# Expert v products of a two-block transformer layer: the weights go into the array and the tokens stream

## The chip, the core and the metric

One core of a Trainium2 chip runs the kernel. TensorE (PE; its weight loads are listed as PEld), VectorE (DVE), ScalarE (ACT), GpSimd (POOL) and SyncE (SP, which issues the DMAs) work side by side and meet at semaphores. The metric is the device time of one execution in microseconds (us); the median of several executions is given. The spread of the executions of this kernel is small, so a change of 0.2% can be told from none.

## What is computed

The program runs two transformer blocks on 256 tokens of width 1024. The change lies in the last layer of the first block and at the start of the second. The first block's feed-forward picks, for every token and each of 8 heads, 16 of 16384 experts; an expert has a row u and a row v of 1024 numbers.

```
def peer_ffn(h, w_query, sub_keys_1, sub_keys_2, expert_u, expert_v):
    ...
        g = jax.nn.softmax(best, axis=-1)
        u = expert_u[idx]
        act = jax.nn.gelu(jnp.einsum('td,thkd->thk', xc, u).astype(jnp.float32), approximate=False)
        w = (g * act).astype(h.dtype)
        return jnp.einsum('thk,thkd->td', w, expert_v[idx])
...
    x = x + peer_ffn(rms_norm(x, ffn_norm_g[layer]), ...)
return rms_norm(x, final_norm_g)
```

The second block begins with two sums over the width of that result, a root-mean-square norm of its own and a product with its first weights (`w_in_e_2`), whose columns feed a short convolution in time.

## The kernel before

**Experts as dense products.** The gather is replaced by products over all experts. They are cut into 64 units of 256 experts. Unit u of index j (`unit_u`, `wstat`, L230) computes gelu(u.x) for 256 experts and 256 tokens. Unit v of index j (`unit_v`, L726) multiplies this by the gate weights `gts`, which a one-hot stage has written to HBM (`gd`) and 16 DMAs of 64 KB bring back for every 4 units, and then by the 256 rows of v (`vstat`, L256). All products are done in three passes of the type float32r: each operand is split into a high part (ACT copy, L77 or L737) and a low part (DVE subtraction, L78 or L738), and high*high, high*low and low*high are summed in PSUM (`mm3`, L82).

**Two ways to place the operands.** In `wstat` the weights are the array's stationary operand, 128x128 at a time, and the tokens stream, 256 columns; one u unit is 48 matmuls of 256 columns (lines L240 to L242). In `vstat` the gated activations `wh`/`wl` are the stationary operand and the rows of v stream, 512 columns; one v unit is 24 matmuls of 512 columns (L83 to L85). Its four accumulators `pv` (tokens x width) fill the four banks of the pool `acc` over all 64 units.

**Order of the work.** A scheduler lays the instructions of each engine out from the program text, and each engine then takes its own list in order. Units u28 to u33 stand one behind the other, then v0, u34, v1, u35 and so on up to u63, v30, and then v31 to v63 alone. The second block's feed-forward (tile names `m`) has the same two kinds of unit: `m_0`*n*`p` (first layer) and `m_1`*n*`p` (second layer) with 48 matmuls of 256 streamed columns, each followed by `m` with 24 of 512.

**Which tokens stream.** In the u units, in the convolution's units `cv0` to `cv5` and in `m_0` the streamed tokens are the tiles `gh`/`gl`; in `m_1` they are `bh`/`bl`. In the built program these tiles begin, in each partition, at byte 22272 and 30464 (`gh`, `gl`), 107680 and 115872 (`bh`, `bl`), and 200864, 202912, 204960 and 207008 (the two buffers each of `wh` and `wl`). The first two are multiples of 64; the others all leave a remainder of 32. The buffers of the split weights (72256, 80448, 88640, 96832) are multiples of 64.

**After v63.** Four DVE additions (L748) put the sum on the residual `x`. Eight PE transposes a half (L92, `prep_half`) turn `x` into width x tokens, ACT and DVE split it (L100, L101), and `cv0` and `cv1` multiply it with the first weights. Beside that `factors` takes the sums of squares (DVE L792, eight ACT passes L794) and a chain of small DVE operations up to `rr` (L803), which `rb` and the convolution's first operation (`cvb`, L831) need. `cv0` uses a bank of the pool `acc`, which the accumulators leave free.

Of the kernel before, what the change touches and what calls it, by code (L numbers as in the profile page):

```python
# [10 lines left out]
F32 = mybir.dt.float32  # L11
# [5 lines left out]
AF = mybir.ActivationFunctionType  # L17
OP = mybir.AluOpType
# [3 lines left out]
P = 128  # L22
T = 256
D = 1024
# [24 lines left out]
def kernel(ctx: ExitStack, tc: tile.TileContext, A: dict, out: bass.AP):  # L49
    nc = tc.nc  # L50
    V, S, PE, GP = nc.vector, nc.scalar, nc.tensor, nc.gpsimd
# [7 lines left out]
    def acc_tile(name):  # L59
        return acc.tile([P, 512], F32, tag="acc", name=name)  # L60

    def mm_tile(name):
        return mmp.tile([P, 512], F32, tag="mm", name=name)
# [18 lines left out]
    def mm3(o, ah, al, bh, bl, start, stop):  # L82
        PE.matmul(o, ah, bh, start=start, stop=False)  # L83
        PE.matmul(o, ah, bl, start=False, stop=False)  # L84
        PE.matmul(o, al, bh, start=False, stop=stop)  # L85

    def prep(src, nk, gain, hi, lo, k0=0, full=None, pool=mm_tile):

        for k in range(nk):
            pt = pool(f"pt{k}")  # L90
            for t in range(2):
                PE.transpose(pt[:, t * P : t * P + P], src[t][:, k * P : k * P + P], ident)  # L92
            if gain is None:
                a = S.activation(hi[:, k0 + k], pt[:, :T], AF.Copy)
                v = V.tensor_sub(lo[:, k0 + k], pt[:, :T], hi[:, k0 + k].bitcast(F32))
            else:
                g = gain(k)
                if full is not None:
                    S.activation(full[:, k0 + k], pt[:, :T], AF.Copy, scale=g)
                a = S.activation(hi[:, k0 + k], pt[:, :T], AF.Copy, scale=g)  # L100
                v = V.scalar_tensor_tensor(lo[:, k0 + k], pt[:, :T], g, hi[:, k0 + k].bitcast(F32), OP.mult, OP.subtract)  # L101
        return a, v
# [71 lines left out]
    def load_ahead(src, n, name, after=(), dst=None):  # L174
        if name not in ahead:
            ahead[name] = load_split(src, n, name, after, dst)
# [8 lines left out]
    def fetch(src, n, name):  # L185
        return ahead.pop(name) if name in ahead else load_split(src, n, name)
# [69 lines left out]
    def vstat(ah, al, src, accs, first, last, name):  # L256

        hi, lo = fetch(src, 2048, name)
        order = [(j, t, nh) for j in range(2) for t in range(2) for nh in range(2)]
        if last:  # L260
            order = [(j, t, nh) for nh in range(2) for t in range(2) for j in range(2)]
        for j, t, nh in order:
            c = slice(j * D + nh * 512, j * D + nh * 512 + 512)
            a = slice(j * T + t * P, j * T + t * P + P)
            mm3(accs[t][nh], ah[:, a], al[:, a], hi[:, c], lo[:, c], first and j == 0, last and j == 1)


    c0 = const.tile([P, C0_COLS], F32, name="c0")
    fin = const.tile([P, D], F32, name="fin")
# [3 lines left out]
    ident = c0[:, C_ID : C_ID + P]  # L273
# [4 lines left out]
    x = [const.tile([P, D], F32, name=f"x{t}") for t in range(2)]  # L278
# [36 lines left out]
    with tc.tile_pool(name="p1", bufs=1) as p1:  # L315
        xh, xl = gh, gl_
# [148 lines left out]
        yT, last_exp = {}, []  # L465
# [67 lines left out]
    with tc.tile_pool(name="p2", bufs=1) as p2, tc.tile_pool(name="gdram", bufs=1, space=bass.MemoryType.DRAM) as gdp:  # L533
        gd = [gdp.tile([P, P, 16], F32, name=f"gd{i}") for i in range(16)]
        xh, xl = gh, gl_
# [8 lines left out]
        def unit_u(n=1, xf=None):  # L544
            for _ in range(n):
                j = nu[0]
                if j == 64:
                    return
                nu[0] += 1
                ps = wstat(xh, xl, A["eu"][j], f"u{j}") if xf is None else wstat_f32(xf, A["eu"][j], f"u{j}")  # L550
                g = p2.tile([P, 512], F32, tag="ga", name=f"ga{j}", bufs=NG)
                S.activation(g, ps, AF.Gelu)
                gact[j] = g
# [3 lines left out]
        with tc.tile_pool(name="p2a", bufs=1) as p2a:  # L557
            rs_f, pr = [], []
# [13 lines left out]
            def split_x():  # L572
                for k in range(0, 8, 2):
                    S.activation(xh[:, k : k + 2], xf[:, k : k + 2], AF.Copy)
                    V.tensor_sub(xl[:, k : k + 2], xf[:, k : k + 2], xh[:, k : k + 2].bitcast(F32))
# [117 lines left out]
        with tc.tile_pool(name="p2c", bufs=1) as p2c:  # L693

            for b in range(16):
                unit_u(1)
                stg = p2c.tile([P, P, 16], F32, tag="stg", name=f"stg{b}", bufs=2)
                for q in range(2):
# [11 lines left out]
                    for g in range(2):  # L710
                        ps = acc_tile(f"gp{b}{q}{g}")
                        for i in range(4):
                            for m in range(2):
                                PE.matmul(ps[:, i * P : i * P + P], oh[0][:, g, :, i], oh[2 + m][:, g, :, i], start=m == 0,  # L714
                                          stop=m == 1)
                        c = q * 8 + g * 4
                        S.activation(stg[:, :, c : c + 4], ps.rearrange("p (t n) -> p n t", t=4), AF.Copy,  # L717
                                     scale=2.0 ** -15)
# [1 line left out]

        p2x.__exit__(None, None, None)
        with tc.tile_pool(name="p2b", bufs=1) as p2b:
            accs = [[acc_tile(f"pv{t}{nh}") for nh in range(2)] for t in range(2)]
            gts = {}

            def unit_v(j):  # L726
                q, jj = divmod(j, 4)
                if jj == 0:
                    gts[q] = p2b.tile([P, 16, 8, 16], F32, tag="gt", name=f"gt{q}", bufs=2)
                    for i in range(16):  # L730
                        nc.sync.dma_start(gts[q][:, i], gd[i][:, 8 * q : 8 * q + 8, :])
                w = gact.pop(j)
                w4 = w.rearrange("p (j g t) -> p j g t", j=2, g=16)
                V.tensor_tensor(w4, w4, gts[q][:, :, 2 * jj : 2 * jj + 2, :].rearrange("p g j t -> p j g t"), OP.mult)  # L734
                wh = p2b.tile([P, 512], F32R, tag="wh", name=f"wh{j}", bufs=2)
                wl = p2b.tile([P, 512], F32R, tag="wl", name=f"wl{j}", bufs=2)
                S.activation(wh, w, AF.Copy)  # L737
                V.tensor_sub(wl, w, wh.bitcast(F32))  # L738
                vstat(wh, wl, A["ev"][j], accs, j == 0, j == 63, f"v{j}")

            unit_u(6)
            for j in range(64):
                unit_v(j)
                unit_u()
            for nh in range(2):
                for t in range(2):
                    c = slice(nh * 512, nh * 512 + 512)
                    V.tensor_add(x[t][:, c], accs[t][nh], x[t][:, c])  # L748


    with tc.tile_pool(name="p3", bufs=1) as p3:
        h = x
        xh, xl = gh, gl_
# [11 lines left out]
        def p4(name, bufs=2, tag=None):  # L765
            return p3.tile([P, 4, P], F32, tag=tag or name[:-1], name=name, bufs=bufs)
# [11 lines left out]
        gg = p3.tile([P, 8], F32, name="gg")  # L778
        V.tensor_mul(gg, gcols[:, G_FIN : G_FIN + 8], gcols[:, G_LME : G_LME + 8])
        rr = sm.tile([P, 2], F32, tag="rr", name="rr")  # L780

        def prep_half(hf):
            c = slice(hf * 512, hf * 512 + 512)
            return prep([x[t][:, c] for t in range(2)], 4, lambda k: gg[:, 4 * hf + k : 4 * hf + k + 1], xh, xl, k0=4 * hf)

        def factors():
            ss4 = sm.tile([P, 2, 2, 2], F32, tag="ss4", name="ss4")
            for hf in range(2):
                for t in range(2):
                    c = slice(hf * 512, hf * 512 + 512)  # L790
                    tt = t1[t][:, c]
                    V.tensor_mul(tt, x[t][:, c], fin[:, c])  # L792
                    for i, z in enumerate((x[t][:, c], tt)):
                        S.activation(mm_tile(f"s3{i}{t}{hf}"), z, AF.Square, accum_out=ss4[:, i, t, hf : hf + 1])  # L794
            ss = sm.tile([P, 4], F32, tag="ss4s", name="ss4s")
            rf = sm.tile([P, 4], F32, tag="rf", name="rf")
            V.tensor_add(ss.rearrange("p (a t) -> p a t", a=2), ss4[:, :, :, 0], ss4[:, :, :, 1])

            V.tensor_scalar(ss, ss, 1.0 / D, None, OP.mult)
            V.tensor_scalar(ss[:, 0:2], ss[:, 0:2], EPS, None, OP.add)  # L800
            V.scalar_tensor_tensor(ss[:, 2:4], ss[:, 0:2], EPS, ss[:, 2:4], OP.mult, OP.add)
            rsqrt(rf, ss, 1.0, 0.0, 4, "rf")
            V.tensor_copy(rr, rf[:, 2:4])  # L803
            scale_row()
            return rf

        rb = p3.tile([P, T], F32, name="rb")
        kqT = p3.tile([P, 8, T], F32, tag="kqT", name="kqT")
        kT, qT = kqT[:, 0:4], kqT[:, 4:8]
        tok = {p: [p4(f"{p}tok{t}", tag="vb" if p == "q" else None) for t in range(2)] for p in "kvq"}  # L810
        ktok, vtok = tok["k"], tok["v"]
        ba = p3.tile([P, 2, 8], F32, name="ba")
# [9 lines left out]
        def conv_mm(u, at=None):  # L822
            return wstat(xh, xl, A["w_conv"][u], f"cv{u}", acc_tile, at)
# [47 lines left out]
        def w_uvz(n):  # L871
            gemm(xh, xl, A["w_uvz"], 8, [(n, k) for k in range(2)], evac_uvz, name="wu")

        prep_half(0)
        pr = []
        cps = [conv_mm(0, lambda: pr.extend(prep_half(1)))]
        load_ahead(A["w_conv"][1], 2048, "cv1", pr)
        rf = factors()
        nc.sync.dma_start(c2, A["c2"])
        V.tensor_copy(nmask, c2[:, C_STR : C_STR + 2 * P].rearrange("p (a b) -> p a b", a=2))  # L880
        V.tensor_scalar(nones, ones, -1.0, None, OP.mult)
# [27 lines left out]
        al = sm.tile([P, 4], F32, tag="al", name="al", bufs=1)  # L909
# [59 lines left out]
        for t in range(2):  # L969
# [4 lines left out]
            for i, (one, col) in enumerate(((nones, gc), (ones, ngc))):  # L974
# [3 lines left out]
                d = p4(f"de{i}{t}", 1)  # L978
# [4 lines left out]
            tt = slice(t * P, t * P + P)  # L983
# [3 lines left out]
            a = p4(f"am{t}")  # L987
# [77 lines left out]
        o = [p4(f"o{t}", tag="w1_1") for t in range(2)]  # L1065
        st = None
        for c in range(4):
            t, r0 = c // 2, c % 2 * 64
# [452 lines left out]
```

## Time and profile before

| | us |
|---|---|
| median of 3 executions | 1773.56 |
| lowest, highest | 1773.37, 1774.61 |
| the profiled execution | 1775.11 |
| its span, first to last instruction | 1773.3 |
| PE busy | 1731.5 (98%) |
| DVE busy | 1132.5 (64%) |
| ACT busy | 886.1 (50%) |

The rows come from the profiled execution, whose clock starts with the span. Matmuls are pipelined: a row gives 0.39 us for one of 512 columns though the next starts 0.23 us later. So times of PE are read here from the starts of units, not from the durations.

### The profile page before, as it was taken

The numbers are of one execution on the slowest core, as the hardware profiler recorded it, in microseconds if no ns is written. First come the engines' busy times: TensorE is split into PE (matmuls) and PEld (weight loads), VectorE is DVE, ScalarE is ACT, GpSimd is POOL, SyncE is SP. The second block draws the span as 40 slices with busy tenths as digits, with TensorE's granted clock in tenths as the row PEclk, the third lists the DMA queues.
The fourth block names the chain that finished last, engine by engine and source line by source line (L and its number), as shares of the span: only waits on it lengthen the run. The fifth ranks groups of instructions, "written<-read, shape, count | busy, mean of one in ns | idle before, by whom it ended". The sixth has DMA issues, their size and how long they took to land.

```text
span 1773.3 us, 26306 instructions
## 1 busy us (share of the span) xinstructions
PE 1731.5 (98%) x10702; PEld 1522.5 (86%) x10702; DVE 1132.5 (64%) x1924; ACT 886.1 (50%) x1156; POOL 22.9 (1%) x22
## 2 busy tenths in 40 slices
PE   8999999999999999999999999999999999999998
PEld 7788899999999999999888888887999787789996
DVE  6646689978646565555555578666555676765555
ACT  5765543544544444444444458545444557554444
POOL 0000000000000000000000000001000001100000
PEclk9999999999999999999999999999999999999999
DMA  6424445465677777775555553215555553345552
GB/s 236 140 96 161 157 156 203 157 227 224 220 246 243 246 250 247 247 239 191 186 184 188 187 185 126 99 50 178 190 189 191 172 182 127 115 171 185 179 185 93
DMA packets 83067, 321.40 MB, mean 181 GB/s; under 512 B 9473, under 2 KB 44545, under 8 KB 47105
## 3 DMA queue, kind: packets, MB, share of 16 engines
q1 hardware_dynamic: 82944, 319.71, 52.9%
q8 instruction: 84, 1.38, 0.3%
q14 instruction: 39, 0.31, 0.0%
HBM read 301.85 MB, written 17.83 MB: 180 GB/s over the span
## 4 chain that ended last, share of the span: by engine, by line
PE 89%; DVE 6%; ACT 3%; issue 1%; DMA 0%; SPq 0%; DVEq 0%; ACTq 0%
PE pv L85 7%; PE pv L83 7%; PE pv L84 7%; PE gp L714 3%; PE m L84 3%; PE m L83 3%; PE m L85 3%; PE wia L83 1%; PE wia L84 1%; PE wia L85 1%; PE pt L92 1%; PE pj L1181 1%; PE wua L85 1%; PE wda L85 1%; PE wda L84 1%
## 5 line engine op out<-in xcount | busy, mean ns | idle before, releaser
L737 ACT ACTIVATE wh<-ga 128x512 fp32r<-128x512 f32 x64 | 40.4, 632 | 194.8 <-PE pv L84 194.8
L738 DVE TENSOR_TENSOR wl<-ga,wh 128x512 fp32r<-128x512 f32 x64 | 44.2, 692 | 90.7 <-ACT wh L737 90.7
L714 PE MATMUL gp<-oh,oh 128*128 128x128 f16 x512 | 63.5, 297 | 0.0
L714 PEld LDWEIGHTS <-oh 128*128 128x128 f16 x512 | 57.5, 117 | 1.5
L1201 ACT ACTIVATE ah<-mr 128x512 fp32r<-128x512 f32 x32 | 20.2, 631 | 76.8 <-DVE mr L1198 76.8
L709 DVE TENSOR_TENSOR oh<-oh,gT 128x1024 f16<-128x1024 f16 x64 | 42.3, 687 | 23.9 <-PE gp L714 23.9
L734 DVE TENSOR_TENSOR ga<-ga,gt 128x512 f32<-128x512 f32 x64 | 41.1, 686 | 2.9 <-DMA gt<-gd 2.8
L1202 DVE TENSOR_TENSOR al<-mr,ah 128x512 fp32r<-128x512 f32 x32 | 22.2, 692 | 21.6 <-ACT ah L1201 21.6
L717 ACT ACTIVATE stg<-gp 128x512 f32<-128x512 f32 x64 | 34.8, 600 | 1.7 <-PE gp L714 1.2
L92 PE MATMUL pt<-c,x 128*128 128x128 f32 x128 | 21.7, 296 | 7.4 <-DMA x<-x 5.9
L92 PEld LDWEIGHTS pt<-c,x 128*128 128x128 f32 x128 | 16.1, 150 | 12.7 <-issue 6.0
L706 DVE TENSOR_TENSOR oh<-iotaR,i1T 128x1024 f16<-128x1024 f16 x32 | 22.1, 689 | 5.1 <-PE gp L714 3.7
L78 DVE TENSOR_TENSOR wiw_0l<-wiw,wiw_0h 128x2048 fp32r<-128x2048 f32 x7 | 16.0, 2292 | 12.7 <-ACT wiw_0h L77 12.7
L100 ACT ACTIVATE gh<-pt,gcols 128x256 fp32r<-128x256 f32 x32 | 13.0, 475 | 19.4 <-PE pt L92 19.4
L84 PE MATMUL wia<-wiw_0l,gh 128*128 128x512 f32 x56 | 22.5, 402 | 0.0
L85 PE MATMUL wia<-wiw_0h,gl 128*128 128x512 f32 x56 | 22.5, 401 | 0.0
L83 PE MATMUL wia<-wiw_0h,gh 128*128 128x512 f32 x56 | 22.3, 404 | 0.0
L83 PE MATMUL wia<-wiw_1h,gh 128*128 128x512 f32 x56 | 22.0, 392 | 0.0
L85 PE MATMUL wia<-wiw_1h,gl 128*128 128x512 f32 x56 | 21.9, 392 | 0.0
L84 PE MATMUL wia<-wiw_1l,gh 128*128 128x512 f32 x56 | 21.9, 392 | 0.0
L1198 DVE TENSOR_TENSOR mr<-mr 128x512 f32<-128x512 f32 x32 | 21.9, 685 | 0.0
L101 DVE SCALAR_TENSOR_TENSOR gl<-pt,gcols,gh 128x256 fp32r<-128x256 f32 x32 | 13.6, 478 | 12.2 <-ACT gh L100 12.2
(2944 smaller groups left out, 6680.2 us busy)
## 6 DMA issues: line engine op xcount, KB each, us to landing
u<-eu SPq DMA_DIRECT2D x64, 1024.0 KB, 4.9
v<-ev SPq DMA_DIRECT2D x64, 1024.0 KB, 4.9
m<-w_mlp SPq DMA_DIRECT2D x64, 1024.0 KB, 4.8
gd<-stg SPq DMA_DIRECT2D x16, 1024.0 KB, 3.9
gt<-gd SPq DMA_DIRECT2D x256, 64.0 KB, 4.4
wiw<-w_in SPq DMA_DIRECT2D x14, 1024.0 KB, 5.4
wdw<-w_qkv SPq DMA_DIRECT2D x12, 1024.0 KB, 4.8
q<-w_query SPq DMA_DIRECT2D x8, 1024.0 KB, 5.1
```

What stands on the lines that cost most here:

```text
L83: PE.matmul(o, ah, bh, start=start, stop=False)
L84: PE.matmul(o, ah, bl, start=False, stop=False)
L85: PE.matmul(o, al, bh, start=False, stop=stop)
L92: PE.transpose(pt[:, t * P : t * P + P], src[t][:, k * P : k * P + P], ident)
L706: V.tensor_tensor(oh[0], io, tok(i1T), OP.is_equal)
L709: V.tensor_tensor(oh[2 + i], oh[1], tok(gT[i]), OP.mult)
L714: PE.matmul(ps[:, i * P : i * P + P], oh[0][:, g, :, i], oh[2 + m][:, g, :, i], start=m == 0, stop=m == 1)
L717: S.activation(stg[:, :, c : c + 4], ps.rearrange("p (t n) -> p n t", t=4), AF.Copy, scale=2.0 ** -15)
L734: V.tensor_tensor(w4, w4, gts[q][:, :, 2 * jj : 2 * jj + 2, :].rearrange("p g j t -> p j g t"), OP.mult)
L737: S.activation(wh, w, AF.Copy)
L738: V.tensor_sub(wl, w, wh.bitcast(F32))
L1202: V.tensor_sub(al, r, ah.bitcast(F32))
```

## The change

The v products now place their operands like the u products: 128x128 blocks of v are stationary, and the gated activations `wh`/`wl` stream with all 256 tokens. The sum so stands as width x tokens, in four banks `yT`, two blocks of 128 of the width in each. It begins with the residual: 16 matmuls of `x` with the identity (`residual_t`) write the transposed `x` into the banks before v0. After v63 ACT and DVE split the banks directly (`split_x`), and ACT also copies them to `xT`; `factors` transposes `xT` back on PE and takes its sums from PSUM.

```diff
+    def vstat_t(ah, al, src, accs, last, name):
+
+        hi, lo = fetch(src, 2048, name)
+        for d in range(8):
+            o = accs[d // 2][:, d % 2 * T : d % 2 * T + T]
+            for j in range(2):
+                c = slice(j * D + d * P, j * D + d * P + P)
+                a = slice(j * T, j * T + T)
+                PE.matmul(o, hi[:, c], ah[:, a], start=False, stop=False, skip_group_check=True)
+                PE.matmul(o, hi[:, c], al[:, a], start=False, stop=False, skip_group_check=True)
+                PE.matmul(o, lo[:, c], ah[:, a], start=False, stop=last and j == 1, skip_group_check=True)
...
-            accs = [[acc_tile(f"pv{t}{nh}") for nh in range(2)] for t in range(2)]
+
+
             gts = {}
+
+            def residual_t():
+                for m in range(4):
+                    for i in range(4):
+                        d, t = 2 * m + i // 2, i % 2
+                        PE.matmul(yT[m][:, i * P : i * P + P], x[t][:, d * P : d * P + P], ident, start=i == 0, stop=False,
+                                  skip_group_check=True)
...
-                vstat(wh, wl, A["ev"][j], accs, j == 0, j == 63, f"v{j}")
+                vstat_t(wh, wl, A["ev"][j], yT, j == 63, f"v{j}")
 
             unit_u(6)
+            yT = [acc_tile(f"pv{m}") for m in range(4)]
+            residual_t()
             for j in range(64):
                 unit_v(j)
                 unit_u()
-            for nh in range(2):
-                for t in range(2):
-                    c = slice(nh * 512, nh * 512 + 512)
-                    V.tensor_add(x[t][:, c], accs[t][nh], x[t][:, c])
...
-        def prep_half(hf):
-            c = slice(hf * 512, hf * 512 + 512)
-            return prep([x[t][:, c] for t in range(2)], 4, lambda k: gg[:, 4 * hf + k : 4 * hf + k + 1], xh, xl, k0=4 * hf)
+        def split_x():
+
+            for m in range(4):
+                for k in (2 * m, 2 * m + 1):
+                    o = yT[m][:, k % 2 * T : k % 2 * T + T]
+                    S.activation(xh[:, k], o, AF.Copy, scale=gg[:, k : k + 1])
+                    V.scalar_tensor_tensor(xl[:, k], o, gg[:, k : k + 1], xh[:, k].bitcast(F32), OP.mult, OP.subtract)
+                last = S.activation(xT[:, 2 * m : 2 * m + 2], yT[m].rearrange("p (k t) -> p k t", k=2), AF.Copy)
+            return last
...
                     tt = t1[t][:, c]
-                    V.tensor_mul(tt, x[t][:, c], fin[:, c])
-                    for i, z in enumerate((x[t][:, c], tt)):
-                        S.activation(mm_tile(f"s3{i}{t}{hf}"), z, AF.Square, accum_out=ss4[:, i, t, hf : hf + 1])
+                    xp = mm_tile(f"xp{t}{hf}")
+                    for k in range(4):
+                        PE.transpose(xp[:, k * P : k * P + P], xT[:, 4 * hf + k, t * P : t * P + P], ident)
+                    V.tensor_mul(tt, xp, fin[:, c])
+                    for i, z in enumerate((xp, tt)):
+                        S.activation(xp, z, AF.Square, accum_out=ss4[:, i, t, hf : hf + 1])
...
-        prep_half(0)
-        pr = []
-        cps = [conv_mm(0, lambda: pr.extend(prep_half(1)))]
+        pr = [split_x()]
+        cps = [conv_mm(0)]
```

On PE the first rows of unit v20 before were these; the name ahead of the arrow is the accumulator, behind it stand the streamed operand and the stationary one, and then the shape of the output.

```order
L83 MATMUL pv00_5098<-v20h_7393,wh20_7387 128x512
L84 MATMUL pv00_5098<-v20l_7394,wh20_7387 128x512
L85 MATMUL pv00_5098<-v20h_7393,wl20_7388 128x512
L83 MATMUL pv01_5099<-v20h_7393,wh20_7387 128x512
L84 MATMUL pv01_5099<-v20l_7394,wh20_7387 128x512
L85 MATMUL pv01_5099<-v20h_7393,wl20_7388 128x512
```

With the change the same place on PE reads:

```order
L275 MATMUL pv0_5440<-wh20_7883,v20h_7889 128x256
L276 MATMUL pv0_5440<-wl20_7884,v20h_7889 128x256
L277 MATMUL pv0_5440<-wh20_7883,v20l_7890 128x256
L275 MATMUL pv0_5440<-wh20_7883,v20h_7889 128x256
L276 MATMUL pv0_5440<-wl20_7884,v20h_7889 128x256
L277 MATMUL pv0_5440<-wh20_7883,v20l_7890 128x256
```

The two operands have changed places, the streamed one is half as wide, and a unit has 48 such rows in place of 24. The tiles `wh` and `wl` keep the byte addresses given above.

On ACT, between v63 and the first weights of the second block, these rows stood before (`gh` is the high part of the transposed sum, `pt` a bank with transposes, `gg` a gain):

```order
L77 ACTIVATE cv0h_9721<-cv0_9719 128x2048
L100 ACTIVATE gh_72<-pt0_9699,gg_9685 128x256
L100 ACTIVATE gh_72<-pt1_9704,gg_9685 128x256
L100 ACTIVATE gh_72<-pt2_9709,gg_9685 128x256
L100 ACTIVATE gh_72<-pt3_9714,gg_9685 128x256
...
L77 ACTIVATE cv1h_9796<-cv1_9794 128x2048
L794 ACTIVATE s3000_9802,ss4_9800<-x0_76 128x512
```

With the change ACT's list there is (`pv0` to `pv3` are the banks of the sum):

```order
L77 ACTIVATE cv0h_11269<-cv0_11267 128x2048
L805 ACTIVATE gh_72<-pv0_5440,gg_11233 128x256
L805 ACTIVATE gh_72<-pv1_5441,gg_11233 128x256
L805 ACTIVATE gh_72<-pv2_5442,gg_11233 128x256
L805 ACTIVATE gh_72<-pv0_5440,gg_11233 128x256
L805 ACTIVATE gh_72<-pv3_5443,gg_11233 128x256
L805 ACTIVATE gh_72<-pv1_5441,gg_11233 128x256
L805 ACTIVATE gh_72<-pv2_5442,gg_11233 128x256
L807 ACTIVATE xT_11237<-pv0_5440 128x512
L807 ACTIVATE xT_11237<-pv1_5441 128x512
L807 ACTIVATE xT_11237<-pv2_5442 128x512
L805 ACTIVATE gh_72<-pv3_5443,gg_11233 128x256
```

The copy of `pv0` to `xT` stands behind seven high parts, one of which reads `pv3`, the bank that v63 fills last. The accumulator of `cv0` gets the bank of `pv0`, and its first matmul waits for that copy.

On PE the 16 transposes between v63 and `cv1`, half of which stood ahead of `cv0` and half among its matmuls, now stand behind `cv0`:

```order
L241 MATMUL cv0p_11273<-gl_73,cv0h_11269 128x256
L242 MATMUL cv0p_11273<-gh_72,cv0l_11270 128x256
L819 MATMUL xp00_11329<-c0_70,xT_11237 128x128 x4
L819 MATMUL xp10_11337<-c0_70,xT_11237 128x128 x4
L819 MATMUL xp01_11345<-c0_70,xT_11237 128x128 x4
L819 MATMUL xp11_11353<-c0_70,xT_11237 128x128 x4
L240 MATMUL cv1p_11395<-gh_72,cv1h_11324 128x256
```

## Rows read from the trace of the kernel before

**Rows 1.** The page's part 4: the chain that ended last, share by engine.
```profile
PE 89%; DVE 6%; ACT 3%; issue 1%; DMA 0%; SPq 0%; DVEq 0%; ACTq 0%
```

**Rows 2.** Busy time by stretch: us, PE, PEld, DVE, ACT, POOL, PEclk, DMA share, GB/s.
```profile
519.00:851.00 332.00, 332.00 (x2159) 299.31 (x2158) 193.49 (x149) 144.84 (x120) 0.00 (x0) 1.00 0.72 237
857.00:1042.00 185.00, 185.00 (x792) 148.71 (x791) 99.34 (x68) 79.62 (x65) 0.00 (x0) 1.00 0.55 187
1080.00:1090.00 10.00, 6.99 (x37) 6.18 (x36) 9.92 (x29) 7.25 (x16) 0.10 (x1) 0.76 0.18 46
1575.00:1735.00 160.00, 160.00 (x993) 143.51 (x992) 83.00 (x57) 69.88 (x58) 0.00 (x0) 1.00 0.55 185
```

**Rows 3.** Timeline of PE, first matmuls of v0, v17, u51, v18: start, us.
```profile
518.46 0.39 PE L83 MATMUL pv<-v0h,wh 128*128 128x512 f32 x1
...
706.93 0.39 PE L83 MATMUL pv<-v17h,wh 128*128 128x512 f32 x1
...
712.55 0.28 PE L240 MATMUL u51p<-gh,u51h 128*128 128x256 f32 x1
...
718.02 0.39 PE L83 MATMUL pv<-v18h,wh 128*128 128x512 f32 x1
```

**Rows 4.** Timeline of PE, first matmuls of u29, u30, u31.
```profile
490.19 0.28 PE L240 MATMUL u29p<-gh,u29h 128*128 128x256 f32 x1
...
495.85 0.28 PE L240 MATMUL u30p<-gh,u30h 128*128 128x256 f32 x1
...
501.50 0.28 PE L240 MATMUL u31p<-gh,u31h 128*128 128x256 f32 x1
```

**Rows 5.** Timeline of PE, the feed-forward's units: ends of m_05p, m_11p, m_112p.
```profile
1260.59 0.28 PE L240 MATMUL m_05p<-gh,m_05h 128*128 128x256 f32 x1
...
1266.06 0.39 PE L83 MATMUL m<-m_05h,ah 128*128 128x512 f32 x1
...
1564.04 0.28 PE L240 MATMUL m_11p<-bh,m_11h 128*128 128x256 f32 x1
...
1569.80 0.28 PE L240 MATMUL m_12p<-bh,m_12h 128*128 128x256 f32 x1
...
1683.50 0.28 PE L240 MATMUL m_112p<-bh,m_112h 128*128 128x256 f32 x1
...
1689.26 0.39 PE L83 MATMUL m<-m_112h,ah 128*128 128x512 f32 x1
```

**Rows 6.** Timeline of PE: matmuls of x with a diagonal, float32, 128 columns.
```profile
209.41 3.81 PE L569 MATMUL ptn<-dgf,x 128*128 128x128 f32 x32 [2.49 <-issue]
```

**Rows 7.** Timeline of PE from v63 to cv2: start, us, count.
```profile
1036.60 0.40 PE L83 MATMUL pv<-v63h,wh 128*128 128x512 f32 x1
...
1042.23 1.04 PE L92 MATMUL pt<-c,x 128*128 128x128 f32 x8
1043.84 0.39 PE L240 MATMUL cv0p<-gh,cv0h 128*128 128x256 f32 x1 [0.57 <-ACT gh L100]
...
1057.82 0.39 PE L240 MATMUL cv2p<-gh,cv2h 128*128 128x256 f32 x1 [0.53 <-ACT cv2h L77]
```

**Rows 8.** Timeline of ACT over the same stretch.
```profile
1043.31 1.57 ACT L100 ACTIVATE gh<-pt,gg 128x256 fp32r<-128x256 f32 x4 [4.59 <-PE pt L92]
...
1049.29 0.61 ACT L794 ACTIVATE s<-x 128x512 f32<-128x512 f32 x1
```

**Rows 9.** Timeline of DVE over the same stretch.
```profile
1054.33 0.16 DVE L797 TENSOR_TENSOR ss4s<-ss 128x4 f32<-128x4 f32 x1 [1.85 <-ACT s L794]
...
1057.60 0.17 DVE L803 COPY rr<-rf 128x2 f32<-128x2 f32 x1
...
1061.26 2.28 DVE L78 TENSOR_TENSOR cv3l<-cv,cv3h 128x2048 fp32r<-128x2048 f32 x1
...
1063.73 0.68 DVE L831 TENSOR_TENSOR cvb<-cv0p,rb 128x512 f32<-128x512 f32 x1
...
1070.75 0.70 DVE L934 TENSOR_SCALAR x<-uv,rf 128x1024 f32<-128x1024 f32 x1
```

More of the change, by code (lines that the diff above doesn't have):

```diff
@@ L807 @@
         rb = p3.tile([P, T], F32, name="rb")
-        kqT = p3.tile([P, 8, T], F32, tag="kqT", name="kqT")
-        kT, qT = kqT[:, 0:4], kqT[:, 4:8]
+        xT = p3.tile([P, 8, T], F32, tag="kqT", name="xT")
         tok = {p: [p4(f"{p}tok{t}", tag="vb" if p == "q" else None) for t in range(2)] for p in "kvq"}
@@ L872, in w_uvz @@
             gemm(xh, xl, A["w_uvz"], 8, [(n, k) for k in range(2)], evac_uvz, name="wu")
-        prep_half(0)
-        pr = []
-        cps = [conv_mm(0, lambda: pr.extend(prep_half(1)))]
+        pr = [split_x()]
+        cps = [conv_mm(0)]
         load_ahead(A["w_conv"][1], 2048, "cv1", pr)
         rf = factors()
+        kqT = p3.tile([P, 8, T], F32, tag="kqT", name="kqT")
+        kT, qT = kqT[:, 0:4], kqT[:, 4:8]
         nc.sync.dma_start(c2, A["c2"])
```

## The prediction

> **What bounds the kernel now.** I read the chain that ended last first: 89% of it is PE [rows 1]. Then the busy time by stretch, for the stretch that is changed: from 519 to 851 us, where u and v units alternate, and from 857 to 1042 us, where v units stand alone, PE is busy without a gap, its granted clock is 1.00 (2.4 GHz), DVE is busy for 58% and 54% and ACT for 44% and 43% [rows 2]. So the time of the expert products is the sum of PE's matmul intervals, and nothing that ACT, DVE or the queues do there shows, as long as it keeps up. Last I read where units start on PE, since durations of pipelined matmuls do not add up. v17 takes 712.55 - 706.93 = 5.62 us for 24 matmuls of 512 columns, 234 ns each; u51 takes 718.02 - 712.55 = 5.47 us for 48 of 256 columns, 114 ns each [rows 3]. From the first v0 to the end of v63 it is 1042.23 - 518.46 = 523.77 us [rows 3, 7]; less 30 u units at 5.475 that leaves 5.62 us for each of 64 v units. Each unit computes the same number of products, so on this alone the new form, which has the shape and the count of a u unit, would gain. The reader is to see that this is not the only interval which the trace has for that shape.
>
> **The v units: which interval.** Three intervals stand in the trace for 48 float32r matmuls of 256 streamed columns, all at clock 1.00. With `gh`/`gl` streaming, u51 takes 5.47 us and m_05p 1266.06 - 1260.59 = 5.47 us [rows 3, 5]. With the same tiles u29 and u30 take 5.66 and 5.65 us [rows 4]. With `bh`/`bl` streaming, m_11p takes 1569.80 - 1564.04 = 5.76 us and m_112p 1689.26 - 1683.50 = 5.76 us [rows 5]. m_05p and m_112p do the same work on the same buffers of split weights and stand in the same alternation with units of 512 columns; what differs is the streamed tile. `gh`/`gl` begin at a byte that is a multiple of 64, `bh`/`bl` 32 bytes past one, and `wh`/`wl`, which now stream, also 32 past one. m_11p follows another unit of 256 columns, as every v unit now does, and it too takes 5.76 us. So the nearest row for the new v unit is m_11p, not u51. I take 5.76: 0.14 us more than now, times 64 is **+9.0 us**. The bounds are u51's 5.47 (-0.15 x 64 = -9.6, or -9.0 with the mean of 5.62 and u's 5.48) and m_11p's own 5.76; u30's 5.655 in between gives +2.3.
>
> The Trainium skill speaks against this reading of the addresses: "SBUF — State Buffer", section Specifications, gives lines of 16 bytes as what an access crosses, and 32 bytes past a multiple of 64 is the start of such a line. By it the new v units would run as u51 does, and the sum of this term would be -9.0 us. No row here shows why `bh`/`bl` stream at 5.76 us; the address is what I find to differ, and it may not be the reason.
>
> **The u units between them.** The 30 units u34 to u63 stand in the same place as before and stream `gh`/`gl`. But this form has two intervals, 5.47 and 5.65, and units that follow one another at 5.65 stay there: u29 and u30 do, and both run at clock 1.00. Now u units follow a v unit that is itself of 256 columns. Below, they stay at 5.475: no cost. Above, all 30 go to 5.655: 30 x 0.18 = +5.4 us. I take 0, since u51 and m_05p enter 5.47 from another form each time, and keep +5.4 as a case of its own.
>
> **The residual at the start.** 16 float32 matmuls of 128 columns stand on PE between u33 and v0, which followed one another without a gap. The same operation with another right side is `x` with a diagonal: 32 in 3.81 us, the last of which ends 0.28 us after it starts, so 3.81 less that pipeline end is 0.11 us each [rows 6]. 16 x 0.11 = **+1.8 us**. Nothing covers it, since PE is the bound there. Below it is nothing only if PE had idled before v0, and it did not. The four DVE additions after v63 go; what they gave back is counted next.
>
> **After v63.** I count from the first matmul of v63 (1036.60) [rows 7]. Before, PE ended v63 at 5.63, ran eight transposes, started `cv0` at 7.24 and `cv2` at 21.22, and `cvb`, behind which DVE works nearly without a gap (9.92 of 10 us between 1080 and 1090 [rows 2]), came at 27.13 [rows 9]. With the change: the last bank is filled at 5.76, ACT sees it at about 6.0, does three high parts at 0.39 (four take 1.57 [rows 8]) and the copy of `pv0` at 0.61, and `cv0`, which waits for that copy, starts at 7.9. **This is a new wait**, and the whole of PE's list stands behind it. `cv0` runs without stops at 5.45 to 13.4; 16 transposes at 0.11 follow to 15.2; `cv1` ends at 20.7, against 21.2. So PE has lost nothing there. But the sums of squares now wait for the transposes, and before them stands the split of `cv2`'s weights, whose buffer is free when `cv0` ends: 13.4 + 2.1 = 15.5. Eight passes at 0.61 [rows 8] end at 20.4, and the chain to `rr` takes 1057.60 - 1054.33 = 3.3 [rows 9]: 23.7, where it was 21.0, 2.7 us later. What DVE does between `rr` and `cvb` changes too: one split of 2.28 (`cv2l`) now stands ahead of `rr`, and the scaling of the second half of `x` (0.70, at 1070.75 before) comes ahead of `cvb` [rows 9]. So `cvb` comes at 27.13 + 2.7 - 2.3 + 0.7 = 28.2, with 0.7 us of later work already done and 0.14 counted with v63: **+0.3**, which I round to **+0.5 us** for one more handover between engines. Bounds: -1 (if PE's start sets the rest) to +2.7 (if the whole delay of `rr` stays). The additions taken away are worth nothing beyond that, since `cv0` waits for ACT in their place.
>
> ACT and DVE hide the rest: a v unit still has one split of weights and one of activations. From 519 to 851 us, 60 units, that is 144.84 / 60 = 2.4 us of ACT and 193.49 / 60 = 3.2 us of DVE a unit [rows 2], within 5.5. No DMA is added or moved.
>
> **Sum.** 9.0 + 1.8 + 0.5 = +11.3 us. On the span of 1773.3 that gives 1784.6, on the execution's own 1775.11 it gives 1786.4; the median of the runs shown lies 1.55 below that execution, so I say **1784.9 us**.
>
> **Rivals.**
> 1. The u units fall to 5.655 too: 11.3 + 5.4 = +16.7, 1790.3. For it: all that follows u28 at that interval stays there [rows 4]. Against: 30 u units now enter 5.47 within their first matmuls after v.
> 2. The new v units run like u51, and the kernel is faster: -9.0 + 1.8 + 0.5 = -6.7, 1766.9. It decides from a v unit below 5.58 us on, where 64 x 0.04 pays for the residual and the end. For it: the same shape, weights and buffers as u. Against: both units named with a tile 32 bytes past a multiple of 64 take 5.76. This is also what the Trainium skill's page named above would make of it.
> 3. The v units run like u30: +2.3 + 1.8 + 0.5 = +4.6, 1778.2. For it: u's second interval needs no odd address. Against: m_05p and m_112p differ though they are entered alike.
> 4. The wait for `pv0` takes the clock down, as two waits of PE near 1082 did: the granted clock was 0.76 over the ten us there [rows 2], 2.4 us of it lost. With it 1787.3. Against: 1.6 us between v63 and `cv0` [rows 7] did not do so before, and 2.1 is not much more.
>
> **How the numbers follow.** Chances: the forecast 0.46, rival 1 0.26, rival 2 0.12, rival 3 0.10, rival 4 alone or more than these 0.06. This kernel's runs tell 0.2% (3.5 us) from no change. Faster by more than that is rival 2, 0.12. Within it, 1770 to 1777, ends the lower half of rival 3: 0.04. Slower is the rest, 0.84. The range leaves out rival 2 and the tails: from 1776, a little under rival 3, to 1793, rival 1 with the upper bound of the end: it holds 0.84. The forecast's own range is 1783 to 1788.
>
> **What would show it.** In the changed kernel's timeline the distance from a v unit's first matmul (L275) to the next unit's first: 5.76 is right, 5.48 is rival 2, 5.65 rival 3. u units 5.48 or 5.65 tell the forecast from rival 1. The 16 rows of L743 should take 1.8 us. `cv0` should wait for ACT about 2.1 us after v63, and `rr` (now L831) should stand 23 to 24 us after v63's start. The prediction is wrong if PE shows gaps inside the v units: then a split that I hold to be hidden is late.

## The result and the profile after

The changed kernel takes 1784.05 us (median of 9 executions, 1782.67 to 1789.84); the kernel before takes 1773.37 us (9 executions, 1770.55 to 1779.67: a spread of 0.5%, where the three ahead of the forecast lay within 0.1%). The ratio is 1.0068, with a 95% interval of 1.0051 to 1.0085: slower, by 9 to 15 us. The forecast was 1784.9.

The profiled execution of the changed kernel took 1782.83 us with a span of 1781.1, 7.7 us above that of before. First its page, part 4, the chain that ended last, to set beside [rows 1]:

```profile
PE 88%; DVE 7%; ACT 3%; issue 1%; DMA 1%; SPq 0%; DVEq 0%; ACTq 0%
```

Then its busy time by stretch, with the columns of [rows 2]: u and v units in alternation, v units alone, and ten us around the first operations of the convolution:

```profile
519.00:857.00 338.00, 338.00 (x2898) 338.00 (x2897) 189.96 (x149) 144.99 (x120) 0.00 (x0) 1.00 0.69 232
861.00:1044.00 183.00, 183.00 (x1527) 183.00 (x1526) 92.61 (x64) 77.13 (x64) 0.00 (x0) 1.00 0.51 183
1080.00:1090.00 10.00, 10.00 (x89) 10.00 (x88) 9.75 (x35) 9.66 (x29) 0.21 (x2) 1.00 0.29 107
```

PE still has no gap in the v stretch, at a granted clock of 1.00, and no split is late. The third row answers to the one of before with 0.76. PE is still the bound; what changed is the distance between its matmuls. The timeline of PE, where v17, u51 and v18 start (as [rows 3]), and u29, u30 and u31 (as [rows 4]):

```profile
708.76 0.28 PE L275 MATMUL pv<-wh,v17h 128*128 128x256 f32 x1
...
714.51 0.28 PE L240 MATMUL u51p<-gh,u51h 128*128 128x256 f32 x1
...
719.97 0.28 PE L275 MATMUL pv<-wh,v18h 128*128 128x256 f32 x1
```

```profile
487.47 0.28 PE L240 MATMUL u29p<-gh,u29h 128*128 128x256 f32 x1
...
492.91 0.28 PE L240 MATMUL u30p<-gh,u30h 128*128 128x256 f32 x1
...
498.35 0.28 PE L240 MATMUL u31p<-gh,u31h 128*128 128x256 f32 x1
```

A v unit takes 5.75 us (5.62 before) and u51 5.46 (5.47 before): the forecast of 5.76 and 5.475. u29 and u30 take 5.44 here and took 5.66 and 5.65 before, though neither the code nor an address of theirs changed. So the same form with the same tiles has two intervals, and one or the other shows in an execution.

The residual, on PE ahead of v0, and the end of v63, on PE, ACT and DVE:

```profile
514.68 3.73 PE L743 MATMUL pv<-c,x 128*128 128x128 f32 x32
518.17 0.36 PE L275 MATMUL pv<-wh,v0h 128*128 128x256 f32 x1
...
1044.52 0.28 PE L275 MATMUL pv<-wh,v63h 128*128 128x256 f32 x1
...
1053.94 0.38 PE L240 MATMUL cv0p<-gh,cv0h 128*128 128x256 f32 x1 [3.50 <-ACT xT L807]
```

```profile
1050.74 2.67 ACT L805 ACTIVATE gh<-pv,gg 128x256 fp32r<-128x256 f32 x7 [4.23 <-DVE gg L797]
1053.25 1.62 ACT L807 ACTIVATE xT<-pv 128x512 f32<-128x512 f32 x3
```

```profile
1050.48 0.17 DVE L797 TENSOR_TENSOR gg<-gcols 128x8 f32<-128x8 f32 x1 [1.64 <-PE pv L277]
...
1071.27 0.17 DVE L831 COPY rr<-rf 128x2 f32<-128x2 f32 x1
...
1075.60 0.69 DVE L858 TENSOR_TENSOR cvb<-cv0p,rb 128x512 f32<-128x512 f32 x1
```

The same execution's busy time in three stretches, from the start of `cv0` to its end (columns as in [rows 2]):

```profile
1053.94:1055.46 1.52, 1.52 (x13) 1.52 (x14) 0.59 (x3) 1.29 (x3) 0.00 (x0) 1.00 0.99 378
1055.46:1058.87 3.41, 3.41 (x19) 3.41 (x18) 1.94 (x4) 3.07 (x3) 0.00 (x0) 0.50 0.35 125
1058.87:1061.10 2.23, 2.23 (x21) 2.23 (x21) 1.64 (x1) 0.96 (x3) 0.00 (x0) 1.00 0.00 0
```

The residual takes 3.49 us. After v63 ACT's seven high parts wait for `gg`, the product of two gains, and `gg` waits for PE's last matmul of v63. From v63's start `cv0` comes at 9.42, `rr` at 26.75 and `cvb` at 31.08 us; before, it was 7.24, 21.00 and 27.13 [rows 7, 9]. PE waited 3.50 us ahead of `cv0`, and 1.5 us into `cv0` the granted clock fell to 0.50 (1.2 GHz) for 3.41 us: **rival 4 did happen here**. `cv0` takes 7.2 us where the forecast had 5.45. This table puts the two executions side by side (us; the end of v63 is its start and one v unit):

| stretch | before | after | difference |
|---|---|---|---|
| up to the end of u33 | 518.46 | 514.68 | -3.78 |
| residual | 0 | 3.49 | +3.49 |
| v0 to the end of v63 | 523.77 | 532.11 | +8.34 |
| end of v63 to `cvb` | 21.50 | 25.32 | +3.82 |
| `cvb` to the end of the span | 709.57 | 705.50 | -4.07 |

### The profile page after: what moved, and what is told of

The parts are those of the page before. It is cut to its first block, busy times and chain, and to the rows that moved or that the text cites. A ratio compares the mean times of both kernels' runs of the same rounds, so it can differ in the third digit from the quotient of the medians.

```text
span 1781.1 us, 29379 instructions
## 1 busy us (share of the span) xinstructions
PE 1734.9 (97%) x12270; PEld 1597.1 (90%) x12270; DVE 1126.4 (63%) x1920; ACT 886.8 (50%) x1160; POOL 22.9 (1%) x22
## 4 chain that ended last, share of the span: by engine, by line
PE 88%; DVE 7%; ACT 3%; issue 1%; DMA 1%; SPq 0%; DVEq 0%; ACTq 0%
PE pv L276 7%; PE pv L277 7%; PE pv L275 7%; PE gp L726 3%; PE m L85 3%; PE m L84 3%; PE m L83 3%; PE wia L84 1%; PE wia L85 1%; PE wia L83 1%; PE pt L92 1%; PE pj L1209 1%; PE wua L85 1%; PE wda L85 1%; PE wda L84 1%
## 5 line engine op out<-in xcount | busy, mean ns | idle before, releaser
L92 PEld LDWEIGHTS pt<-c,x 128*128 128x128 f32 x112 | 14.1, 151 | 12.3 <-issue 5.7
L78 DVE TENSOR_TENSOR wdw_0l<-wdw,wdw_0h 128x2048 fp32r<-128x2048 f32 x6 | 13.7, 2292 | 11.9 <-ACT wdw_0h L77 11.9
```

## The experiments

The question left by the result was why 5.75: I had found that the tiles with that interval begin 32 bytes past a multiple of 64, and no more. **The theory** was the address; **the rivals** were the form of the unit (six matmuls on one accumulator, then the next), the region of the memory, and that the tile is written anew for each unit. Times below are medians of all executions of a kernel; the times of units come from its profiled execution.

**e1, wh/wl at a multiple of 64** (and **e4, at 48 past one**). The edits to the changed kernel:

```diff
         with tc.tile_pool(name="p2b", bufs=1) as p2b:
+            p2b.tile([P, 8], F32, name="pad")
```

```diff
-                wh = p2b.tile([P, 512], F32R, tag="wh", name=f"wh{j}", bufs=2)
+                wh = p2b.tile([P, 528], F32R, tag="wh", name=f"wh{j}", bufs=2)[:, 4:516]
...
```

> The changed kernel with 32 bytes of padding ahead of wh/wl, so that the streamed tiles begin at a multiple of 64 bytes and nothing else moves. If the address is the reason for the 5.75 us, a v unit takes 5.46 to 5.48 us as a u unit does: 64 x 0.28 = 18 us less than the changed kernel, 1766 us. If the place or the use of the tiles is the reason (two buffers written anew for each unit) or the address plays no part, 5.75 stays, and so does the time, 1784 us.

> The changed kernel with wh/wl beginning 48 bytes past a multiple of 64. If what counts is whether a tile begins at a multiple of 64, v units stay at 5.75 and the time at 1784 us. If the distance counts and 32 is the worst, they fall between 5.46 and 5.75, 1766 to 1784 us. If a start off 32 costs again beside a start off 64, they rise above 5.75: at twice the rise 6.04, 1802 us.

e1: 1783.13 us, ratio to before 1.0057 (1.0036 to 1.0077); e4: 1783.3 us, 1.0058 (1.0041 to 1.0075). Units of e1 on PE:

```profile
708.81 0.28 PE L275 MATMUL pv<-wh,v17h 128*128 128x256 f32 x1
...
714.51 0.28 PE L240 MATMUL u51p<-gh,u51h 128*128 128x256 f32 x1
```

A v unit takes 5.70 us in e1 and 5.65 in e4. At a multiple of 64 a unit is 0.05 us shorter, not 0.29, and longer than at 48 past one. As I had stated it, the theory fell. In e4 the u units between, whose tiles did not move, stand at 5.45 and 5.65 in turn, so its 5.65 may be the second interval of [rows 4] and not the address's own.

**e2 and e8, the kernel before with the same padding**, of wh/wl alone and ahead of all stages:

> The kernel before with the same 32 bytes of padding, so that wh/wl, which there are the stationary operand, begin at a multiple of 64. If only the streamed operand's address counts: 5.62 us a v unit as before, 1773.4 us. If the stationary operand's counts too, a v unit falls to about 5.5 us (matmuls of 512 columns with gh/gl stationary stand 4 ns closer than those with wh/wl, 24 x 4 = 0.1 us): 64 x 0.1 = 6 to 7 us less, 1767 us.

> The kernel before with 32 bytes of padding ahead of all stages, so that wh/wl, ah/al, mh/ml and bh/bl all begin at a multiple of 64 bytes. e2 showed 0.04 us a v unit for wh/wl alone. If the remainder has to do with the 5.76 us of the m_1 units, these 16 units fall to between 5.47 and 5.70: 1 to 5 us less, and the 16 + 16 units that hold ah/al some tenths each: 1763 to 1769 us. If not: as e2, 1769 us.

e2: 1768.84 us, 0.9977 (0.9961 to 0.9992), a v unit 5.577 against 5.617. e8: 1766.03 us, 0.9963 (0.9949 to 0.9977), an m_1 unit 5.70 against 5.76. So the stationary operand's address counts too, and a multiple of 64 isn't all of it there either.

**e5, the v units stream gh/gl** (the gate and the activations are left out of the sum):

```diff
-                vstat_t(wh, wl, A["ev"][j], yT, j == 63, f"v{j}")
+                vstat_t(gh.rearrange("p k t -> p (k t)"), gl_.rearrange("p k t -> p (k t)"), A["ev"][j], yT, j == 63, f"v{j}")
```

> The changed kernel, but the matmuls of the v units stream the first two blocks of gh/gl in place of wh/wl, which are still made (the gate and the activations are left out of the sum). Stationary blocks, banks and order stay. e1 took the remainder by 64 out of question as the whole reason, so three theories are left. If it is the streamed tile all the same (where it lies, by something else than that remainder): 5.46 us a v unit, 1766 us. If it is the form of the unit (six matmuls into one half of a bank and then the next, against 24 in a u unit; weight blocks 512 bytes apart against 1024): 5.70 to 5.76 us and 1783 us. If it is that the streamed tile is written anew for each unit: 5.46 too, so this run does not tell that from the first.

```profile
705.86 0.28 PE L240 MATMUL u50p<-gh,u50h 128*128 128x256 f32 x1
...
711.30 0.28 PE L275 MATMUL pv<-gh,v17h 128*128 128x256 f32 x1
...
716.74 0.28 PE L240 MATMUL u51p<-gh,u51h 128*128 128x256 f32 x1
```

v17 and u50 both take 5.44 us. So it is the streamed tile that decides; by which of its properties, this run doesn't say. The profiled execution took 1768.43; the eight executions lie from 1765 to 1768 (three) and from 1781 to 1788 (five). Those of the second group have no trace; that their units run at 5.65, as u29 did in [rows 4], would fit, and isn't shown.

**e6, u units in short runs.** Each writes six matmuls into one half of its bank, then six into the other:

```diff
-        for j in range(2):
-            for k in range(8):
...
+        for i in range(16):
+            j, k = i // 2 % 2, i // 4 * 2 + i % 2
...
```

> The changed kernel, but each unit of the u form writes six matmuls into one half of its bank, then six into the other, as a v unit does, instead of 24 and 24. If the form of the unit is the reason for 5.75: u units rise from 5.46 to about 5.75, and the 86 units that stream gh/gl cost 25 us, 1808 us. If not: 5.46 and 1784 us.

u units stay at 5.46 us: the form is not the reason. The time, 1789.35 us (two executions), is 5 us above the changed kernel's median all the same; v0 starts at 527.05 there against 518.17, so the loss lies ahead of the units in question. In that stretch the granted clock of e6 fell to 0.50 twice, for 6.8 us each (from 115.25 and from 210.83), and that of the changed kernel not once; this is worth 6.8 us at most, and where the rest comes from stays open.

**e9, tiles at a multiple of 256**, where `gh`/`gl` are, and **e13, 128 bytes further** (56 columns for 24):

```diff
         with tc.tile_pool(name="p2b", bufs=1) as p2b:
+            p2b.tile([P, 24], F32, name="pad")
...
     with tc.tile_pool(name="p4", bufs=1) as p4_:
         h = x
+        p4_.tile([P, 24], F32, name="pad4")
         bh = p4_.tile([P, 8, T], F32R, name="bh")
```

> The changed kernel with 96 bytes of padding ahead of the tiles of the v units and of the last stage, so that wh/wl and bh/bl, ah/al begin at a multiple of 256 bytes, as gh/gl do; they lie 96 bytes from where they were. e5 showed that the streamed tile makes the difference, e1 and e8 that a multiple of 64 isn't enough. If a remainder by more than 64 (128 or 256) is what counts: v units 5.44 to 5.47 us, m_1 units 5.47, 1784 - 18 - 5 = 1761 us. If it is the region in which the tile lies (gh/gl below byte 40000, the slow ones above 107000), or that it is written anew: 5.70 for the v units, m_1 over 5.7, 1782 us.

> The kernel of e9 with 128 bytes more of padding: wh/wl and bh/bl, ah/al begin 128 past a multiple of 256. If a multiple of 128 is what counts: v units 5.44 us and the time of e9, 1758 us. If it is a multiple of 256: v units 5.6 to 5.76 us, 1775 to 1784 us.

e9: 1758.43 us, 0.9929 (0.9908 to 0.995). e13: 1783.76 us, 1.0058 (1.0035 to 1.0081). Their units, e9 first:

```profile
704.92 0.28 PE L275 MATMUL pv<-wh,v17h 128*128 128x256 f32 x1
...
710.36 0.28 PE L240 MATMUL u51p<-gh,u51h 128*128 128x256 f32 x1
...
715.80 0.28 PE L275 MATMUL pv<-wh,v18h 128*128 128x256 f32 x1
```

```profile
711.04 0.28 PE L275 MATMUL pv<-wh,v17h 128*128 128x256 f32 x1
...
716.70 0.28 PE L240 MATMUL u51p<-gh,u51h 128*128 128x256 f32 x1
...
722.35 0.28 PE L275 MATMUL pv<-wh,v18h 128*128 128x256 f32 x1
```

In e9 a v unit takes 5.44 us and an m_1 unit 5.47, though they lie in the same region and are used as before: neither the region nor the rewriting is the reason. In e13 v17 takes 5.66 and u51, whose tiles did not move, 5.65. That is the second interval, which `gh`/`gl` alone have too [rows 4]; all four executions of e13 lie within 1783.4 to 1784.1. In its last stage, where `bh`/`bl` stream from a remainder of 128, the units start so on PE:

```profile
1574.80 0.28 PE L240 MATMUL m_11p<-bh,m_11h 128*128 128x256 f32 x1
...
1580.24 0.28 PE L240 MATMUL m_12p<-bh,m_12h 128*128 128x256 f32 x1
...
1585.68 0.39 PE L83 MATMUL m<-m_12h,ah 128*128 128x512 f32 x1
...
1591.27 0.28 PE L240 MATMUL m_13p<-bh,m_13h 128*128 128x256 f32 x1
...
1596.93 0.40 PE L83 MATMUL m<-m_13h,ah 128*128 128x512 f32 x1
```

m_11p and m_12p take 5.44 us, m_13p and all behind it 5.65. So a tile at a remainder of 128 has the same two intervals as one at 0, the short one too, and not the 5.75 of before.

**e10, gh/gl 32 bytes past a multiple of 256**, by laying a tile of gains ahead of them (e3, an earlier form with the same aim, gave no result):

```diff
+    gcols = const.tile([P, G_COLS], F32, name="gcols")
     gh = const.tile([P, 8, T], F32R, name="gh")
     gl_ = const.tile([P, 8, T], F32R, name="gl")
-    gcols = const.tile([P, G_COLS], F32, name="gcols")
```

> What e3 was meant to be: the changed kernel with gh/gl at 22816 and 31008, 32 bytes past a multiple of 64 and of 256, and all else where it was. If a remainder (by 64 or by 256) counts: u units 5.7 to 5.76 us, with the convolution's and m_0 units 86 x 0.29 = 25 us more, 1809 us. If the region counts: 5.46 and 1784 us.

```profile
721.35 0.28 PE L275 MATMUL pv<-wh,v17h 128*128 128x256 f32 x1
...
727.10 0.28 PE L240 MATMUL u51p<-gh,u51h 128*128 128x256 f32 x1
...
732.78 0.28 PE L275 MATMUL pv<-wh,v18h 128*128 128x256 f32 x1
```

1804.03 us (two executions), 1.0176 (1.0153 to 1.0199); u51 takes 5.68 and m_0 units 5.67. The fast tile becomes slow in its own region, 544 bytes further on, at a remainder of 32. The 5.68 is only 0.03 above the second interval of the tile where it was; what speaks for the address is that every u unit from u28 on and every m_0 unit from m_02p on stands there, and that both executions are 20 us longer.

**e11, the kernel before with the padding of e9:**

> The kernel before with the padding of e9. There wh/wl are the stationary operand. If a multiple of 256 counts for it too: v units 5.5 us against 5.577 at a multiple of 64 (e2), and m_1 units 5.47: 1773 - 8 - 5 = 1760 us. If only a multiple of 64 counts for it: 5.577; then m_1 alone tells, 1766 us or 1770 us.

1756.0 us, 0.9902 (0.9884 to 0.992): a v unit takes 5.50 us and an m_1 unit 5.47, while the u units of the profiled execution stand at 5.66.

**e7, the waits after v63 taken away**, and **e12, that and the padding of e9**:

```diff
+            gg = gcols[:, G_FIN : G_FIN + 8]
+            V.tensor_mul(gg, gg, gcols[:, G_LME : G_LME + 8])
             gts = {}
...
-        gg = p3.tile([P, 8], F32, name="gg")
-        V.tensor_mul(gg, gcols[:, G_FIN : G_FIN + 8], gcols[:, G_LME : G_LME + 8])
...
-            return wstat(xh, xl, A["w_conv"][u], f"cv{u}", acc_tile, at)
+            return wstat(xh, xl, A["w_conv"][u], f"cv{u}", acc_tile if u else mm_tile, at)
```

> The changed kernel with the two waits at the end of v63 taken away: the gains gg are multiplied before the v units, in memory that nothing had used before, and cv0 gets a bank of the other pool, so it doesn't wait for the copy of pv0. If these two waits are the 3.7 us between v63 and cv0: cv0 starts within 1 us of the end of v63, and the kernel is 2 to 4 us faster, 1781 us. If the sums of squares behind it (rr 26.8 us after v63's start) set the end all the same: under 1 us, 1784 us.

> The changed kernel with both repairs: the padding of e9 and the two waits of e7 taken away. If they add up: e9's 1758.4 less the 3.4 us by which cvb came earlier in e7, 1755 us, as fast as the kernel before with that padding (e11, 1756 us) or a little faster. If the end after v63 is set by something else once v63 ends earlier: 1758 us.

PE and DVE of e7, the start of v63, of `cv0`, and `cvb`:

```profile
1044.05 0.28 PE L275 MATMUL pv<-wh,v63h 128*128 128x256 f32 x1
...
1049.81 0.28 PE L240 MATMUL cv0p<-gh,cv0h 128*128 128x256 f32 x1
```

```profile
1071.77 0.69 DVE L858 TENSOR_TENSOR cvb<-cv0p,rb 128x512 f32<-128x512 f32 x1
```

`cv0` follows v63 without a gap, and `cvb` comes 27.72 us after v63's start, 3.36 earlier than in the changed kernel. (The order on PE is new too: four of the transposes stand among `cv0`'s matmuls.) Not all of the 3.36 is the waits'. In e1, which has both waits, the clock stays at 1.00 in `cv0`, which takes 5.56 us there (the row of its busy time, then PE and DVE):

```profile
1051.39:1056.95 5.56, 5.56 (x48) 5.56 (x49) 3.13 (x6) 4.98 (x7) 0.00 (x0) 1.00 0.48 171
```

```profile
1042.03 0.28 PE L275 MATMUL pv<-wh,v63h 128*128 128x256 f32 x1
...
1051.39 0.39 PE L240 MATMUL cv0p<-gh,cv0h 128*128 128x256 f32 x1 [3.50 <-ACT xT L808]
```

```profile
1071.52 0.68 DVE L859 TENSOR_TENSOR cvb<-cv0p,rb 128x512 f32<-128x512 f32 x1
```

Counted from the end of v63, `cvb` comes at 25.3 in the changed kernel, 23.8 in e1 and 22.0 in e7. So the two waits, with the order that hangs on them, cost 1.8 us, and the fall of the clock behind them 1.5. By its profiled execution e7 is 3.75 us faster (1779.08); its four executions scatter from 1779.08 to 1788.01 (median 1784.39), so the timing alone doesn't show the gain. e12 takes 1752.78 us, 0.9891 (0.9869 to 0.9913), with the v units and the u units between them at 5.44. It beats both kernels, by 19 us the one before; against e11, which keeps the old form, the intervals overlap, and no difference is shown.

## Why the forecast came out, step by step

**The v units: right in size, half right in reason.** 64 units rose from 5.617 to about 5.755, +8.8 us against +9.0; with u units 0.5 us shorter in sum, the stretch grew by 8.34. The step that found the interval, m_11p as the nearest row and not u51, holds: e5 shows that the streamed tile decides, e6 that the form does not. The remainder by which I explained it was wrong: at a multiple of 64 the unit still takes 5.70 (e1), at one of 256 it takes 5.44 (e9), and `gh`, which is at a multiple of 256, slows down when it is moved off (e10). So rival 2 failed by the address alone: with 96 bytes of padding its unit time comes true. The rule that spoke against me, lines of 16 bytes in the Trainium skill ("SBUF — State Buffer", section Specifications), is not borne out as the whole: all starts tried were multiples of 16, and units took from 5.44 to 5.76 us.

**The u units between them: right.** 5.46 against 5.475; rival 1 did not happen in the profiled execution. The executions of 1789.4 to 1789.8 (three of nine) have no trace, but their mean granted clock is 0.993 to 0.995 against 0.997 to 0.999 in the other six. The second interval needs no fall of the clock: u29 and u30 of before had it at 1.00. So the clock explains these three better than rival 1.

**The residual: mis-sized by half.** I read "x32" in [rows 6] as 32 matmuls of the program. A float32 matmul stands as two rows in the trace (a transpose as one): the 16 of the residual are x32 and take 3.49 us, not 1.8. [Rows 6] showed 3.81 us for the 16 of `x` with the diagonal, and the same subtraction would have given 3.5.

**After v63: the step that failed.** I let four high parts be done before v63 ended, and `cv0` start at 7.9. But `gg` has a place in memory that the stage of v63 gives back only with its last matmul, so nothing of ACT's began before 6.2, seven parts stood ahead of the copy of `pv0`, and `cv0` came at 9.42. That is 1.5 us of delay. Then rival 4 came true: with the clock at 0.50 for 3.41 us `cv0` ended 1.7 us later still. So `rr` came at 26.75 and not at 23.7, `cvb` at 31.08 and not at 28.2: +3.8 us for my +0.5, outside my bounds of -1 to +2.7. e7 has neither the waits nor the fall, and there the stretch is 0.5 us above that of before. I gave rival 4 2.4 us and a chance of at most 0.06; it cost 1.5, and it does not follow the wait each time, as e1 shows. Before, the additions of v63 stood ahead of `gg` on DVE and waited for PE, so that `gg` had no wait of its own.

**Why the sum was near all the same: luck.** Two terms were 1.7 and 3.3 us too small, and the clock of the execution before, which I had as my base, made up for it. Its trace has the clock at 0.50 in four stretches, beside one at its very end; that of the changed kernel has, beside its end, only the one in `cv0`. The four (columns as in [rows 2]):

```profile
68.12:71.53 3.41, 3.41 (x11) 2.58 (x10) 0.61 (x2) 2.91 (x8) 0.00 (x0) 0.50 0.78 269
115.91:119.32 3.41, 3.41 (x16) 3.13 (x15) 1.44 (x6) 1.34 (x6) 0.00 (x0) 0.50 0.52 137
1085.29:1092.12 6.83, 6.83 (x34) 6.83 (x33) 5.76 (x10) 6.28 (x26) 0.00 (x0) 0.50 0.58 199
1750.89:1754.30 3.41, 3.41 (x9) 2.64 (x10) 2.09 (x1) 1.26 (x1) 0.00 (x0) 0.50 0.00 0
```

Of the -3.78 ahead of the residual, 1.3 is u28 to u33 at 5.44 for 5.66; the other 2.5 lie about the first two of these stretches, in stages that the change does not touch. Of the -4.07 after `cvb`, 2.97 are gained up to the split `wuw_0l` (1107.67 before, 1116.57 after), about the third, and 1.50 from the last stage's `x` (1736.20, 1745.50) to the end, about the fourth. The medians, which the forecast was of, hide part of this: the profiled execution of before lies 1.7 us above its median of nine, that of after 1.2 below. Set side by side at the same mean granted clock, 0.999, eight executions of before (listed with the later runs) take 1768.3 to 1771.2 us and three of the changed kernel 1782.7 to 1783.2. That is 13.3 us in the mean, near the 14.1 of the residual, the v stretch and the end without the fall (3.49 + 8.34 + 2.3), and 2 more than I had forecast.

## What to carry to other kernels

Look up where the streamed and the stationary tile of the costliest products begin: moving them to a multiple of 256 bytes took the changed form from 1784.05 to 1758.43 us and the old one 1.0% below itself, more than the change of form was worth either way. Price an operation from a row with the count of the program beside the count of the trace. When work is moved to the end of a stage, see whether small operands of the next stage lie in memory that the stage still holds. Before two executions are compared stage by stage, find the stretches with a lower granted clock in both: here they stood behind most of the difference in stages that the change does not touch.

## What was not expected of the hardware

The interval of float32r matmuls depends on the address of the streamed tile. For 48 matmuls of 256 columns, by the remainder of that address by 256:

| remainder | tile, kernel | us a unit |
|---|---|---|
| 0 | `gh`/`gl`, before; `wh`/`wl`, e9 | 5.44 to 5.48, or 5.65 |
| 32 | `gh`/`gl`, e10 | 5.68 |
| 48, 112, 176, 240 (the four tiles) | `wh`/`wl`, e4 | 5.65 (the u units between: 5.45 and 5.65 in turn) |
| 128 | `wh`/`wl` and `bh`/`bl`, e13 | 5.65; 5.44 in two units |
| 160 | `wh`/`wl`, after; `bh`/`bl`, before | 5.75, 5.76 |
| 192 | `wh`/`wl`, e1; `bh`/`bl`, e8 | 5.70 |

At a remainder of 0 there are two steady intervals, 5.44 and 5.65 us, and both occur in one execution: in e9 the units u29 to u33 and m_0 stood at 5.65, the v units at 5.44. A remainder of 128 has both as well. What chooses between them stays open, and with it whether a tile at 128 would hold the short one as e9's did. The split weights, stationary in all these units, began at a remainder of 64 in every run; whether the streamed tile's address counts by itself or by its distance from theirs was not tried. The stationary operand counts too: with `wh`/`wl` there a unit of 24 matmuls of 512 columns took 5.62 us at 160, 5.58 at 192 (e2) and 5.50 at 0 (e11), and with `ah`/`al` there 5.60 at 128 (e13).
